# A hybrid attention/Fourier/Hyena layer: the Hyena filter constants loaded after the second modulation block, their products and sums one block later

## The chip, the cores and the metric

The kernel runs on one core of a Trainium2 chip. The metric is the device time of one execution in microseconds (us), the median of several runs. The engines of the core work side by side: TensorE (PE in the profile, its weight loads PEld), VectorE (DVE), ScalarE (ACT), GpSimd (POOL) and SyncE (SP), whose queue issues nearly all the loads here.

## The reference, cut to what matters

One layer for 128 context tokens and 256 latent tokens, width 2048, all in float32:

```python
ada = silu(cvec) @ w_ada + b_ada                 # 2048 x 6144: shift, scale, gate
h   = rmsnorm(x, norm_g) * (1 + scale) + shift
proj = h @ w_in                                  # attention, Fourier, Hyena inputs, gates
# Hyena branch: its long filters do not depend on x
f = sin(f_freq * (z @ f_w1 + f_b1)); f = sin(f_freq * (f @ f_w2 + f_b2))
f = (f @ f_w3) * exp(-t * deltas)                # f_w3: 64 x 2048; the decay window
f = f / (sum_t |f| + eps)                        # one sum for context, one for latents
kf = rfft(two-sided filter)                      # as products with DFT matrices here
y = x + gate * (merge(att, fourier, hyena(kf)) @ w_out)
```

## The kernel before

The products with the large weights are made in three passes of split float32 parts: each weight tile `w` (256 rows x 512 columns, 512 KB) is cast to `wh` on ACT (line 533) and its remainder `wl` taken on DVE (line 535); then `h_hi*wh`, `h_lo*wh` and `h_hi*wl` are summed. One such tile against all 384 tokens is a pair of row blocks, 24 matmuls of 384 columns for the Hyena columns.

The modulation (`ada`) is made in five blocks of its 2 x 2048 shift and scale columns (`ADA`, line 106): blocks 0 and 1 of 256 columns, blocks 2 to 4 of 512. Each block reads its part of `w_ada` (8 tiles of 512 KB in two DMAs each for blocks 0 and 1, 16 tiles of 512 KB for the others) through four buffers, two tiles to a step of matmuls (called an ada step below). Behind the last step a chain makes that block's `h`: a copy of the row (line 461), transposes on PE (464), bias and gain (474, 476), then per row block and token group one DVE instruction (485), one on ACT for `h_hi` (486) and one on DVE for `h_lo` (488). The end of a block is the event `h0` ... `h4`.

The first large products, of the Hyena columns (`hc_part`), go by `GROUPS` (line 108): group 0 needs only `h0` (four weight tiles), group 1 only `h1` (four), group 2 `h2` (eight), and so on; the partial sums of group 0 are copied out by ACT (line 695), those of the later groups added by DVE (line 697). Then come the Fourier columns (`u`), their gate (`gateB`), and the attention columns.

The filters (`filters`, line 599) are a flow of their own: two small sine layers, then the last layer's 12 products (line 626: two matmuls of 512 columns each, and a multiply by the decay window `win` on DVE, line 627), which need `f_w3` (`fw3`, two loads of 512 KB) cast and split in `split_w3` (lines 608, 609) and `win` (768 KB); the sums of absolute values (638), their reciprocals (640, 642), a spread of the row over all partitions (two matmuls for each of four rows, line 647, "spread rows" below) and a multiply (649); then six DFT steps with the split matrices `fwd_hi`, `fwd_lo` from the first 256 KB of `blob`. The Hyena convolution waits for `hc`, `filters` and `ada`; the attention columns wait for its first half (`conv0`).

All these flows are woven by a planner (`Weave`, lines 131 to 191) while the program is written: each step has an assumed cost on PE, a due time and events that it waits for; ready steps are taken by priority (ada 0, filters 2, Hyena 3, `main` 9). The order so found is the order of PE and of SP's queue; ACT and DVE are ordered by the scheduler of the framework after `h0`. An order once written is kept: an engine that waits for one instruction holds up all behind it.

Of the kernel before, what the change touches and what calls it, by code (L numbers as in the profile page):

```python
# [48 lines left out]
LATENT, CONTEXT = 0, 1  # L49
# [144 lines left out]
def step(pe, lat=0.0, after=(), wait=0.0, pace=0, count=0, at=0.0):  # L194
    return dict(pe=pe, lat=lat, after=after, wait=wait, pace=pace, count=count, at=at)
# [4 lines left out]
MM2 = 0.44  # L200
# [7 lines left out]
def hybrid_block(ctx: ExitStack, tc: tile.TileContext, a: dict):  # L208
# [28 lines left out]
    def tmp(name, shape=None, dt=F32):  # L237
        return work.tile(shape or [P, 512], dt, tag="tmp", name=name, bufs=6)

    def acc():  # L240
        return ps_acc.tile([P, 512], F32, tag="acc", name="acc")

    def aux():
        return ps_aux.tile([P, 512], F32, tag="aux", name="aux")

    def mm(out, lhsT, rhs, start=True, stop=True):
        nc.tensor.matmul(out, lhsT, rhs, start=start, stop=stop)  # L247
# [24 lines left out]
    def filter_constants(*which):  # L272
        for n in which:
            W.load((1, 1, 1.5, 0.5)[n] * LOAD)
            if n < 2:
                nc.sync.dma_start(out=fw3[n], in_=a["f_w3"][:, 1024 * n:1024 * n + 1024])
            elif n == 2:
                nc.sync.dma_start(out=win, in_=a["win"])
            else:
                nc.sync.dma_start(out=blob[:, 0:N_FWD], in_=a["blob"][:, 0:N_FWD])  # L280
# [127 lines left out]
    def ada_load():  # L408
        b, kt = next(ada_order, (None, None))
        if b is None:  # L410
            return
        _, c0, wd, *_ = (b, *ADA[b])
        nk = 512 // wd
        if b == 0 and kt // nk >= N_ADA:
            w = s6([P, nk, 2, wd], F32, "w_ada")
        else:
            w = adap.tile([P, nk, 2, wd], F32, tag="ada", name="w_ada", bufs=N_ADA)
        rows = w_ada[P * kt:P * kt + P * nk, 0:2 * D].rearrange("(k p) (t c) -> p k t c", p=P, t=2)
        for k in range(nk):
            nc.sync.dma_start(out=w[:, k], in_=rows[:, k, :, c0:c0 + wd])  # L420
        ada_loads.append((w, W.load(LOAD)))
# [3 lines left out]
    def ada(b, c0, wd, pace, rate):  # L425

        nk, nh, hw = 512 // wd, wd // 256, wd // 2
        pa = None
        n = 1 if b == 0 else 2
        if b == 0:  # L430
            for i in range(KT // nk):
                if i == KT // nk - 1:
                    prefetch(1)
                ada_load()
            prefetch(2)
            filter_constants(0, 1)
        if b == 1:
            yield step(0.0, pace=0.4)
            for _ in range(N_ADA):
                ada_load()  # L440
        for i in range(0, KT // nk, n):
            if b == 0 and i == 6:
                W.signal("ada0")
            yield step(0.26 + 0.43 * n * (nk * wd / 512), at=ada_loads[n - 1][1], pace=pace + rate * nk * i)
            pa = pa or acc()
            ws = [ada_loads.pop(0)[0] for _ in range(n)]
            for k in range(n * nk):
                kt = nk * i + k
                for j in range(4):
                    mm(pa[32 * j:32 * j + 32, 0:hw], cond[:, kt, :],  # L450
                       ws[k // nk][:, k % nk, j // 2, hw * (j % 2):hw * (j % 2) + hw], kt == 0, kt == KT - 1)
            if b > 0:
                for _ in range(n):
                    ada_load()
        if b == 0:
            ahead.append(weights(w_in, 0, OFF_HC))
            next(ahead[0])
        yield step(nh * TR, lat=0.6, after=("x",), wait=1.0)
        with tc.high_priority():
            row = tmp("ada_row")  # L460
            nc.vector.tensor_copy(out=row[:, 0:hw], in_=pa[:, 0:hw])
            pt = aux()
            for i in range(nh):
                nc.tensor.transpose(out=pt[:, P * i:P * i + P], in_=row[:, P * i:P * i + P], identity=ident)
            v = pt[:, 0:hw].rearrange("p (h t r q) -> p t q r h", h=nh, t=2, r=2)
            k0 = c0 // P
            ksl = slice(k0, k0 + wd // P)

            def rh(x):
                return x.rearrange("p (r h) -> p r h", r=2)  # L470

            for m, t, bias in ((am, 1, bsc), (sm, 0, bsh)):
                for s in range(2):
                    nc.vector.tensor_tensor(out=rh(m[:, s, ksl]), in0=v[:, t, s], in1=rh(bias[:, ksl]), op=ALU.add)
            for s in range(2):
                nc.vector.tensor_tensor(out=am[:, s, ksl], in0=am[:, s, ksl], in1=ng[:, ksl], op=ALU.mult)
            g = k0 // 4
            if k0 % 4 == 0:
                hh[g] = s6([P, 4, TOK], F32R, f"h{g}_hi")
                hl[g] = s6([P, 4, TOK], F32R, f"h{g}_lo")  # L480
            parts = [(xT[g][:, kt % 4, sl], hh[g][:, kt % 4, sl], hl[g][:, kt % 4, sl], rstd_b[:, sl],
                      am[:, s, kt:kt + 1], sm[:, s, kt:kt + 1])
                     for kt in range(k0, k0 + wd // P) for s, sl in ((LATENT, LSL), (CONTEXT, CSL))]
            for x, hi, lo, r, scale, shift in parts:
                nc.vector.scalar_tensor_tensor(out=x, in0=x, scalar=scale, in1=r, op0=ALU.mult, op1=ALU.mult)  # L485
                nc.scalar.activation(hi, x, AF.Identity, bias=shift)
            for x, hi, lo, r, scale, shift in parts:
                nc.vector.scalar_tensor_tensor(out=lo, in0=x, scalar=shift, in1=hi.bitcast(F32), op0=ALU.add,  # L488
                                               op1=ALU.subtract)
        if b == 0:  # L490
            ahead[0] = [next(ahead[0])]
        W.signal(f"h{b}")
# [24 lines left out]
    def prefetch(n):  # L517

        while len(loaded) < min(n, len(order)):
            src, kp, c0 = order[len(loaded)]  # L520
            w = stage.tile([P, 2, 512], F32, tag="w", name="w", bufs=N_W)
            nc.sync.dma_start(out=w, in_=src[256 * kp:256 * kp + 256, c0:c0 + 512].rearrange("(k p) c -> p k c", p=P))
            loaded.append((w, W.load(LOAD)))
# [75 lines left out]
    def filters():  # L599
# [13 lines left out]
        mm(p2[:, 0:TOK], fw2, f1)  # L613
        f2 = yield from sin_layer(p2, P, 10, "f2")
        f2s = split(f2, tmp("f2h", None, F32R)[:, 0:TOK], tmp("f2l", None, F32R)[:, 0:TOK])
        yield step(0.0, pace=0.1)
        filter_constants(2, 3)
        fw3s = [split_w3(x) for x in fw3]
        hw = [s6([P, NT, HW], F32, f"hw{j}") for j in range(4)]
        for jj, t in ((0, 0), (0, 1), (0, 2), (2, 0), (2, 1), (2, 2)):  # L620
            for j in (jj, jj + 1):
                yield step(MM2, lat=0.3, after=("h0",), wait=7.0)
                ph = aux()
                ts_, cs_ = slice(P * t, P * t + P), slice(512 * (j % 2), 512 * (j % 2) + 512)
                for i, f in enumerate(f2s):
                    mm(ph, f[:, ts_], fw3s[j // 2][:, cs_], i == 0, i == 1)
                nc.vector.tensor_tensor(out=hw[j][:, t, :], in0=ph, in1=win[:, t, :], op=ALU.mult)
        split(blob[:, 0:N_FWD].rearrange("p (q c) -> p q c", q=4), fwd_hi, fwd_lo)
        for s, ts in ((CONTEXT, (0,)), (LATENT, (1, 2))):
            pz = aux()  # L630
            for t in ts:
                yield step(0.0, lat=1.0)
                ab = [tmp("habs") for _ in range(4)]
                for j in range(4):
                    nc.scalar.activation(ab[j], hw[j][:, t, :], AF.Abs)
                yield step(1.0, lat=2.2, after=("h1" if s == CONTEXT else "h2",))
                for j in range(4):
                    mm(pz[32 * j:32 * j + 32, :], ones, ab[j], t == ts[0], t == ts[-1])
            r = tmp("hrec")
            nc.vector.tensor_scalar(out=r, in0=pz, scalar1=EPS, scalar2=None, op0=ALU.add)  # L640
            for c in range(4):
                nc.vector.reciprocal(out=r[:, P * c:P * c + P], in_=r[:, P * c:P * c + P])
            rh, rl = split(r, tmp("rh", None, F32R), tmp("rl", None, F32R))
            for j in range(4):
                yield step(MM2, lat=7.5 if j == 0 else 0.5)
                pb = aux()
                bcast_row(pb, 32 * j, rh, rl)
                for t in ts:
                    nc.vector.tensor_tensor(out=hw[j][:, t, :], in0=hw[j][:, t, :], in1=pb, op=ALU.mult)  # L649
# [507 lines left out]
```

## Time and profile before

| | us |
|---|---|
| median of 3 runs | 1303.23 (1303.11 to 1303.71) |
| the profiled execution | 1304.65, of which the span from first to last instruction 1302.9 |
| PE busy / DVE / ACT / POOL | 1282.2 (98%) / 736.9 (57%) / 469.3 (36%) / 27.6 (2%) |
| mean granted clock of PE | 0.997 |
| chain that ended last, by engine | PE 95%, DMA 2%, DVE 1%, ACT 1% |

PE bounds the kernel: a microsecond is gained or lost only where PE waits, or where its clock is at the lower level. The busy share of PE counts a matmul from its start to its modelled end, so it hides short waits; the waits are read from the order of the instructions in time.

### The profile page before, as it was taken

How to read it: one execution, taken by the hardware profiler on the slowest of the kernel's cores; microseconds unless marked ns; L12 is line 12 of the kernel's file. 1: busy time of each engine (PE TensorE's matmuls, PEld its weight loads, DVE VectorE, ACT ScalarE, POOL GpSimd, SP SyncE). 2: the span in 40 equal slices, each digit the busy share in tenths (PEclk: the TensorE clock that was granted, in tenths of full speed). 3: DMA queues.
4: the chain of work that ended last, by engine and by line, in shares of the span. 5: the costliest groups of instructions: out<-in, count | busy, mean ns of one | idle time of the engine just before them, and what ended most of it. 6: DMA issues, size and time to landing. Idle time of an engine off the chain costs nothing.

```text
span 1302.9 us, 16835 instructions
## 1 busy us (share of the span) xinstructions
PE 1282.2 (98%) x6602; PEld 1073.9 (82%) x6602; DVE 736.9 (57%) x1164; ACT 469.3 (36%) x736; POOL 27.6 (2%) x66
## 2 busy tenths in 40 slices
PE   7989999999999999999999999999999999999998
PEld 5857889889788988889888888888888888888886
DVE  4767767674775245542453766566656653454443
ACT  5432445322324344533444233323333333242221
POOL 0000000000000000000000000000000000010000
PEclk9999999999999999999999999999999999999999
DMA  9897853433434455444553555555555554464542
GB/s 337 299 324 268 278 179 114 116 111 97 113 97 138 146 125 114 123 132 123 124 110 114 180 176 171 185 170 178 173 183 161 176 157 129 141 189 133 157 150 86
DMA packets 118864, 210.95 MB, mean 162 GB/s; under 512 B 16385, under 2 KB 24961, under 8 KB 118785
## 3 DMA queue, kind: packets, MB, share of 16 engines
q1 hardware_dynamic: 116192, 202.13, 51.8%
q0 software_dynamic: 2448, 7.61, 1.8%
q8 instruction: 52, 0.85, 0.3%
q14 instruction: 28, 0.22, 0.1%
q10 hardware_dynamic: 144, 0.14, 0.0%
HBM read 205.65 MB, written 4.19 MB: 161 GB/s over the span
## 4 chain that ended last, share of the span: by engine, by line
PE 95%; DMA 2%; DVE 1%; ACT 1%; SPq 0%; issue 0%
PE acc L247 87%; PE aux L247 6%; DMA w_ada<-in_w_ada 2%; PE aux L846 0%; PE aux L1073 0%; PE aux L927 0%; SPq L365 0%; DVE hc L697 0%; DVE wl L535 0%; DVE h_lo L488 0%; PE aux L726 0%; ACT wh L533 0%; DVE xT L485 0%; SPq L420 0%; DVE hw L649 0%
## 5 line engine op out<-in xcount | busy, mean ns | idle before, releaser
L533 ACT CAST wh<-w 128x1024 fp32r<-128x1024 f32 x272 | 286.5, 1053 | 699.3 <-PE acc L247 634.7
L535 DVE TENSOR_TENSOR wl<-w,wh 128x1024 fp32r<-128x1024 f32 x272 | 332.3, 1223 | 364.1 <-PE acc L247 266.4
L247 PE MATMUL acc<-wh,h_hi 128*128 128x512 f32 x912 | 362.4, 397 | 0.6 <-ACT gateA L806 0.6
L247 PE MATMUL acc<-wh,h_lo 128*128 128x512 f32 x912 | 355.9, 390 | 0.0
L247 PE MATMUL acc<-wl,h_hi 128*128 128x512 f32 x912 | 240.0, 395 | 0.0
L247 PEld LDWEIGHTS acc<-wh,h_hi 128*128 128x128 f32 x912 | 171.3, 188 | 37.4 <-issue 1.4
L247 PEld LDWEIGHTS acc<-wh,h_lo 128*128 128x128 f32 x912 | 171.3, 188 | 35.7 <-issue 1.4
L247 PEld LDWEIGHTS acc<-wl,h_hi 128*128 128x128 f32 x912 | 168.6, 188 | 35.2 <-issue 1.9
L247 PE MATMUL acc<-h_lo,wh 128*128 128x384 f32 x448 | 151.3, 338 | 3.6 <-DVE h_lo L488 3.6
L247 PE MATMUL acc<-h_hi,wh 128*128 128x384 f32 x448 | 152.6, 341 | 0.1
L1008 DVE SCALAR_TENSOR_TENSOR gate_part<-w_gate,cond,gate_part 128x512 f32<-128x512 f32 x120 | 84.7, 749 | 27.2 <-DMA w_gate<-in_w_ada 27.2
L247 PE MATMUL acc<-h_hi,wl 128*128 128x384 f32 x448 | 91.9, 339 | 0.0
L247 PEld LDWEIGHTS acc<-h_hi,wh 128*128 128x128 f32 x448 | 84.5, 189 | 7.3 <-issue 5.5
L247 PEld LDWEIGHTS acc<-h_lo,wh 128*128 128x128 f32 x448 | 84.6, 189 | 5.6 <-DVE h_lo L488 4.7
L247 PEld LDWEIGHTS acc<-h_hi,wl 128*128 128x128 f32 x448 | 78.3, 188 | 5.9 <-issue 3.6
L247 PE MATMUL acc<-wh,m_hi 128*128 128x512 f32 x192 | 75.0, 390 | 0.0
L247 PE MATMUL acc<-wh,m_lo 128*128 128x512 f32 x192 | 74.7, 389 | 0.0
L247 PE MATMUL acc<-wl,m_hi 128*128 128x512 f32 x192 | 49.6, 390 | 0.0
L247 PEld LDWEIGHTS acc<-wh,m_lo 128*128 128x128 f32 x192 | 36.1, 188 | 7.4
L247 PEld LDWEIGHTS acc<-wh,m_hi 128*128 128x128 f32 x192 | 36.0, 188 | 7.4
L247 PEld LDWEIGHTS acc<-wl,m_hi 128*128 128x128 f32 x192 | 36.0, 188 | 7.4
L697 DVE TENSOR_TENSOR hc<-acc,hc 128x384 f32<-128x384 f32 x64 | 31.5, 550 | 16.8 <-PE acc L247 16.7
(253 smaller groups left out, 1197.7 us busy)
## 6 DMA issues: line engine op xcount, KB each, us to landing
w<-in_w_in SPq DMA_DIRECT2D x208, 512.0 KB, 3.8
w_ada<-in_w_ada SPq DMA_DIRECT2D x48, 512.0 KB, 5.7
w<-in_w_br SPq DMA_DIRECT2D x32, 512.0 KB, 4.1
w_gate<-in_w_ada SPq DMA_DIRECT2D x64, 256.0 KB, 4.2
w<-in_w_out SPq DMA_DIRECT2D x32, 512.0 KB, 3.9
w_ada<-in_w_ada SPq DMA_DIRECT2D x32, 256.0 KB, 7.0
x<-in_x_sample SPq DMA_DIRECT2D x4, 512.0 KB, 8.8
bm<-in_rpb SPq DMA_DIRECT2D x32, 64.0 KB, 7.4
```

Source lines behind the costliest of these rows:

```text
L247: nc.tensor.matmul(out, lhsT, rhs, start=start, stop=stop)
L533: nc.scalar.copy(out=wh, in_=w)
L535: nc.vector.tensor_tensor(out=wl, in0=w, in1=wh.bitcast(F32), op=ALU.subtract)
L697: nc.vector.tensor_tensor(out=hc[i][:, j, :], in0=ps, in1=hc[i][:, j, :], op=ALU.add)
L1008: nc.vector.scalar_tensor_tensor(out=part[s], in0=w, scalar=cond[:, kt, s:s + 1], in1=before, op0=ALU.mult, op1=ALU.add)
```

## The change

The loads of `fw3` are taken out of block 0 of the modulation, and all four constant loads (`fw3` twice, `win`, `blob`; 2 MB) are issued by the filters' flow 0.5 planned us after `h1`. The 12 products wait for `h1` plus 17 planned us where they waited for `h0` plus 7. The context's sums wait for `h2` (before `h1`), the latents' for `h3` (before `h2`). The diff in full:

```diff
@@ -433,7 +433,6 @@
                     prefetch(1)
                 ada_load()
             prefetch(2)
-            filter_constants(0, 1)
         if b == 1:
             yield step(0.0, pace=0.4)
             for _ in range(N_ADA):
@@ -613,13 +612,13 @@
         mm(p2[:, 0:TOK], fw2, f1)
         f2 = yield from sin_layer(p2, P, 10, "f2")
         f2s = split(f2, tmp("f2h", None, F32R)[:, 0:TOK], tmp("f2l", None, F32R)[:, 0:TOK])
-        yield step(0.0, pace=0.1)
-        filter_constants(2, 3)
+        yield step(0.0, after=("h1",), wait=0.5)
+        filter_constants(0, 1, 2, 3)
         fw3s = [split_w3(x) for x in fw3]
         hw = [s6([P, NT, HW], F32, f"hw{j}") for j in range(4)]
         for jj, t in ((0, 0), (0, 1), (0, 2), (2, 0), (2, 1), (2, 2)):
             for j in (jj, jj + 1):
-                yield step(MM2, lat=0.3, after=("h0",), wait=7.0)
+                yield step(MM2, lat=0.3, after=("h1",), wait=17.0)
                 ph = aux()
                 ts_, cs_ = slice(P * t, P * t + P), slice(512 * (j % 2), 512 * (j % 2) + 512)
                 for i, f in enumerate(f2s):
@@ -633,7 +632,7 @@
                 ab = [tmp("habs") for _ in range(4)]
                 for j in range(4):
                     nc.scalar.activation(ab[j], hw[j][:, t, :], AF.Abs)
-                yield step(1.0, lat=2.2, after=("h1" if s == CONTEXT else "h2",))
+                yield step(1.0, lat=2.2, after=("h2" if s == CONTEXT else "h3",))
                 for j in range(4):
                     mm(pz[32 * j:32 * j + 32, :], ones, ab[j], t == ts[0], t == ts[-1])
             r = tmp("hrec")
```

## Rows read from the trace of the kernel before

**Rows 1.** Stretches: us; busy us (instructions) of PE, PEld, DVE, ACT, POOL; clock; DMA share; GB/s.
```profile
95.00:100.00 5.00, 2.52 (x7) 1.96 (x7) 4.41 (x11) 0.80 (x2) 0.00 (x0) 0.65 0.95 259
100.00:105.00 5.00, 5.00 (x33) 2.48 (x33) 1.26 (x2) 0.00 (x0) 0.00 (x0) 0.67 0.83 292
```

**Rows 2.** PE in time, around h2: start, us, line, operation [idle before, releaser].
```profile
87.61 1.29 PE L247 MATMUL acc<-w_ada,cond 128*32 128x256 f32 x16
...
89.95 1.07 PE L247 MATMUL aux<-habs,ones 128*32 128x512 f32 x8
...
97.48 0.69 PE L247 MATMUL acc<-h_lo,wh 128*128 128x384 f32 x1 [3.25 <-DVE h_lo L488]
```

**Rows 3.** DVE in time, around h2.
```profile
88.97 0.42 DVE L461 COPY ada_row<-acc 128x256 f32<-128x256 f32 x1 [1.32 <-PE acc L247]
...
93.03 1.95 DVE L697 TENSOR_TENSOR hc<-acc,hc 128x384 f32<-128x384 f32 x4 [0.43 <-PE acc L247]
94.90 1.22 DVE L535 TENSOR_TENSOR wl<-w,wh 128x1024 fp32r<-128x1024 f32 x1
...
96.69 2.72 DVE L488 SCALAR_TENSOR_TENSOR h_lo<-xT,sm,h_hi 128x256 fp32r<-128x256 f32 x8
```

**Rows 4.** PE in time, around h1.
```profile
57.35 0.43 PE L247 MATMUL acc<-w_ada,cond 128*32 128x128 f32 x8 [0.32 <-DMA w_ada<-in_w_ada]
...
58.52 0.27 PE L464 MATMUL aux<-first,ada_row 128*128 128x128 f32 x1
...
60.58 1.66 PE L247 MATMUL acc<-h_hi,wl 128*128 128x384 f32 x8
```

**Rows 5.** PE in time, the context's spread rows.
```profile
68.73 0.50 PE L247 MATMUL aux<-rh,ident_r 128*128 128x512 f32 x1 [1.11 <-ACT rh L308]
69.46 0.50 PE L247 MATMUL aux<-rl,ident_r 128*128 128x512 f32 x1 [0.23 <-DVE rl L309]
```

**Rows 6.** SP's queue in time: the filter loads and block 1's first loads.
```profile
22.72 0.94 SPq L276 DMA_DIRECT2D fw<-in_f_w  x2
...
27.67 9.49 SPq L420 DMA_DIRECT2D w_ada<-in_w_ada  x8
```

**Rows 7.** Stretches: the hole in the loads.
```profile
41.00:46.00 5.00, 5.00 (x52) 4.17 (x51) 4.55 (x7) 2.87 (x6) 0.00 (x0) 1.00 0.39 123
```

**Rows 8.** PE in time, around h0 (matmuls on `first` alone are fillers).
```profile
27.35 0.72 PE L247 MATMUL acc<-w_ada,cond 128*32 128x128 f32 x16
...
30.79 0.44 PE L247 MATMUL acc<-h_hi,wh 128*128 128x384 f32 x1
31.54 0.44 PE L247 MATMUL acc<-h_lo,wh 128*128 128x384 f32 x1 [0.31 <-DVE h_lo L488]
```

**Rows 9.** PE in time, one filter product between two pairs of group 0's matmuls.
```profile
42.14 0.39 PE L247 MATMUL aux<-fw3hl,f2h 128*128 128x512 f32 x1
...
42.60 0.51 PE L247 MATMUL acc<-h_hi,wl 128*128 128x384 f32 x2
```

**Rows 10.** The instructions on tile hw: duration ns min/median/max, first and last start.
```profile
L627 DVE TENSOR_TENSOR hw<-aux,win x12: 684/692/693, 38.6 to 51.2; 128x512 f32<-128x512 f32 x12
```

**Rows 11.** DVE in time, the latents' reciprocals.
```profile
103.71 0.69 DVE L640 TENSOR_SCALAR hrec<-aux 128x512 f32<-128x512 f32 x1 [4.30 <-PE aux L247]
...
109.63 0.69 DVE L309 TENSOR_TENSOR rl<-hrec,rh 128x512 fp32r<-128x512 f32 x1 [0.69 <-ACT rh L308]
```

**Rows 12.** The instructions on tiles hc and specC, as rows 10.
```profile
L697 DVE TENSOR_TENSOR hc<-acc,hc x64: 547/548/558, 66.6 to 235.0; 128x384 f32<-128x384 f32 x64
...
L683 ACT COPY specC<-aux x2: 570/571/572, 160.0 to 200.2; 1x512 f32<-1x512 f32 x2
```

**Rows 13.** PE in time, the transposes of block 3.
```profile
138.56 0.38 PE L464 MATMUL aux<-first,ada_row 128*128 128x128 f32 x2
```

**Rows 14.** The chain that ended last: start, us, what (the end of `conv0`).
```profile
302.46 1.34 PE aux L247 x12
303.79 7.98 PE acc L247 x46
```

## The prediction

> **What bounds the kernel now.** I read first the page's busy shares and the chain that ended last: PE carries the end nearly everywhere, so only PE's waits and its clock count. Then I read PE's busy time and clock by stretches and the instructions in time where PE is not full. The reader should see that past 32 us PE loses time in few places, and that nearly all the large ones lie before 105 us, where the change works. They are: at the last ada step of block 1 PE waits 0.3 us for `w_ada` [rows 4]; at the context's spread rows 1.1 + 0.2 us for the reciprocals [rows 5]; at `h2` 3.25 us for `h_lo` [rows 2]. [...] Together 0.3 + 1.3 + 3.25 + 2.9 = 7.8 us. That is all that the change can win there.
>
> The `h2` wait has a cause worth seeing. The chain from the row copy (88.97) to the first `h_lo` that PE needs (97.48) is 8.5 us long because DVE, in its written order, first waits for and adds group 1's last sums (0.43 + 1.95) and makes a `wl` (1.22) [rows 3]. Without them it is 8.5 - 3.6 = 4.9 us.
>
> **What the change does, part by part.**
>
> *Loads.* 2 MB leave SP's queue ahead of block 1 (the fw loads stand at 22.7, block 1's at 27.7) [rows 6] and stand behind block 2's first four tiles. Of their own they cost PE nothing: the queue has a hole of about 3 us here, a DMA share of 0.39 over five us [rows 7], because block 1's next loads wait for PE to free buffers. Block 1 is ready sooner, and its DMA wait (0.3 us) goes. The same bytes still stand ahead of block 2's last tile, so `h2` gains little from the loads. They can't delay the products, which are due 17 planned us after `h1`; behind SP's four issues only block 2's and the weights' loads queue, and those have four tiles ahead.
>
> *Products.* 12 at 42.60 - 42.14 = 0.46 us [rows 9] are 5.5 us of PE work that leave the stretch from `h0` to `h1` and enter that from `h1` to `h2`. PE's sum is the same; only the holes count.
>
> *The hole at `h1`.* Going through the planner's costs by hand, block 1's last ada step now comes after all of group 0 (before, group 0's last `wl` products stood behind it and, with the context's sums and an ada step, covered the chain: group 0 ends at 60.58 + 1.66 = 62.2, with no idle time noted on the way from 57.8 [rows 4]). Nothing ready is left: group 1 needs `h1`, the products are not due, block 2's first step stands behind group 1's first matmuls. The chain's length is read at `h0`, where fillers cover it: from the end of the ada step (27.35 + 0.72) to the first matmul that needs `h_lo` (31.54) is 3.5 us [rows 8]. Less the transposes (0.27) and one early matmul, about 3.0 us of new idle. From below, 1.5 if the scheduler and a late load let group 0's matmuls fall behind; from above 4.5, the way from that ada step's end to group 1 before (57.78 to 62.24) [rows 4]. I take 3.0, from the nearest row, an equal chain.
>
> *From `h1` to `h2`.* Group 1, eight ada steps, and now the products. DVE has to multiply each product by the window (12 x 0.69 = 8.3 us) [rows 10] where in group 0 it had little else; in group 1 it also adds the sums (0.55 each, four to a weight tile) [rows 12] and makes `wl` (1.22) [rows 3]. By their due times the products run beside two weight tiles: 8.3 + 8 x 0.55 + 2 x 1.22 = 15.1 us of DVE, against 2 x 24 x 0.173 (7.98 us for 46 matmuls) [rows 14] + 5.5 = 13.8 us of PE, or 15.1 with one ada step of 1.3 [rows 2] among them. DVE falls behind by 1.3 us or not at all, and PE waits where its auxiliary PSUM buffers run out. Bounds 0 and 2.5 (two such overhangs); I take 0.6, the middle of the first two.
>
> *The hole at `h2`.* By the plan all of group 1 and all products are done before block 2's last two ada steps, so DVE's chain is free of the two foreign pieces: 4.9 us (above), of which PE fills 0.4 with transposes [rows 13], 1.1 with the context's sums and 1.3 with block 3's first step [rows 2]. 2.1 us of idle in place of 3.25. Bounds: 1 (more cover left) and 5 (the foreign pieces again).
>
> *Sums.* The context's spread rows move behind `h2`. Their chain on DVE starts only after the longer `h2` chain. From the first reciprocal instruction to `rl` it takes 109.63 + 0.69 - 103.71 = 6.6 us [rows 11]; it can begin when the last `h_lo` is done, 2.0 us after PE restarts (six of eight instructions in 2.72) [rows 3]; PE reaches the spread rows 6.5 us after its restart (line 645 has them 7.5 planned us behind the sums, which end 1.0 after `h2`, and group 2 starts 2.0 after it). So PE waits about 2 + 6.6 - 6.5 = 2.1 for `rl`, and a little more for what DVE interleaves: I take 2.6 (bounds 0.5 and 4), where it was 1.3 at `h1` [rows 5]. The latents' spread rows behind `h3` meet a full group 2 and the same chain as before: nothing either way, up to 1.
>
> *Clock.* A hole of 3.25 us brought 6.8 us of half speed [rows 1, 2]; a wait of 1.3 us [rows 5] brought none, as the page's mean clock of 0.997 has room for little beside that spell. The new holes of 3.0, 2.1 and 2.6 lie between. I take one spell, 2.9 us (bounds none, and two: 5.8).
>
> [...]
>
> **The sum.** New: 3.0 + 0.6 + 2.1 + 2.6 + 2.9 = 11.2; gone: 7.8; so 3.4 us longer. On the profiled execution's 1304.65 that gives 1308.0; this one lies 1.4 over the median, so for the median 1303.2 + 3.4 = 1306.6.
>
> **The rivals.**
>
> *No spell of low clock.* The same holes, all too short or too broken. For it: only one of two waits in the trace was followed by a spell. Against: three holes, not one. 11.2 - 2.9 - 7.8 = 0.5 us longer: 1303.7.
>
> *Faster: the products cover `h2` and the holes shrink.* If group 1's last matmuls or some products slip behind block 2's last ada step, they stand beside the chain, as group 1's did before, while DVE's foreign pieces are gone; `h1` comes with some of group 0 left, and the spread rows wait no more than before. 1.5 + 0 + 1.5 + 1.3 = 4.3 and no spell, against 7.8: 3.5 us less, 1299.7. It decides from the point where block 1's last tile lands before group 0's last weight tile is done in PE's order, so that about 1.5 us of work is behind it. For it: block 1's loads start some 5 us sooner [rows 6]. Against: the order is fixed by planned times, not by when loads land.
>
> *Two spells, or the filters come too late.* The latents' sums move from 89.95 to about 138.6 [rows 2, 13], 49 us, less some 9 of stall and half speed that lay in the chain before; filters that were done at 200 would be done at about 240, against the last sums of `hc` at 235.0 [rows 12]. The Hyena branch then starts some 5 us late. Its first half has 8.0 us of `main`'s work left behind it [rows 14], after which PE would have nothing but the attention columns, and they wait for `conv0`. So 5 us are hidden; past 8 each further us is lost on PE. With 3 lost there, or with a second spell: 1306.6 + 2.9 = 1309.5.
>
> *A queue held by a late filter load.* The casts of `fw3` (lines 608, 609) stand in ACT's and DVE's order; if they stand ahead of group 1's sums while `fw3` is still in flight, everything behind waits. Up to 2 us, inside the range above.
>
> **How the numbers follow.** One spell, 1306.6: 0.40. No spell, 1303.7: 0.28. Faster, 1299.7: 0.17. Two spells or late filters, 1309.5: 0.15. A measurement of this kernel can tell about 0.2%, 2.6 us, from no change. Each case has an error of some 2 us: of the first, six tenths lie over 1305.8; of the second, eight tenths lie within; of the third, seven tenths lie under 1300.6. Faster 0.12 + 0.03 = 0.15; slower 0.24 + 0.03 + 0.15 = 0.42; within 0.43. The range takes in most of the third and the fourth: 1299.6 to 1310.4. The likeliest case's own range is 1304.6 to 1308.6.
>
> **What would show it.** PE's order should have all of group 0 ahead of block 1's last ada step, and then a wait of about 3 us for `h_hi` and `h_lo`, near 54 to 57 us, where before it was full. Group 1 should begin about 5 us sooner than at 62.2. The last ada step of block 2 should stay near 88 to 91, with DVE's chain behind it near 5 us and no `hc` or `wl` inside it; the spread rows should wait 2 to 3 us near 103. From 250 us on every instruction of `main` should be later by one and the same amount. It is wrong if the `h1` hole is under 1.5 us, if the granted clock stays at 1.00 up to 110 us, if DVE holds PE for more than 2.5 us among the products, or if PE waits between 300 and 320.

## The result, and the profile after

| | before | changed |
|---|---|---|
| median, us | 1303.47 (1303.11 to 1304.45) | 1311.27 (1310.13 to 1311.54) |
| ratio | | 1.0053, 95% interval 1.0042 to 1.0065 |
| profiled execution, and its span | 1304.65, 1302.9 | 1311.54, 1309.8 |
| PE busy | 1282.2 | 1284.2 |

The change costs 0.5%, 6.9 us by the ratio (the two medians differ by 7.8): slower, as forecast, but about twice the 3.4 us of the sum. That is the upper end of the range: 1.0053 times the 1303.2 of the forecast is 1310.1, against 1310.4, and the median itself lies 0.9 past it. Matmul by matmul, the large products of the two profiles stand 6.9 us apart from the last sums of `hc` (near 240 us) to the end; beyond 200 us PE's two longest waits are the same in both (0.7 for `pT`, 0.6 for `gateA`), none between 300 and 320. So all of it was lost ahead of the Fourier columns, and the reading goes by the places of the forecast.

PE around `h1` in the changed kernel (start, us, line, operation, idle before and its releaser); it answers to [rows 4]:

```profile
52.96 1.08 PE L247 MATMUL acc<-w_ada,cond 128*32 128x128 f32 x32
54.60 0.33 PE L463 MATMUL aux<-first,ada_row 128*128 128x128 f32 x1 [0.57 <-DVE ada_row L460]
56.81 0.44 PE L247 MATMUL acc<-h_hi,wh 128*128 128x384 f32 x1 [1.88 <-ACT h_hi L485]
57.56 0.45 PE L247 MATMUL acc<-h_lo,wh 128*128 128x384 f32 x1 [0.31 <-DVE h_lo L487]
```

0.57 + 1.88 + 0.31 = 2.8 us of idle, where group 0's last products had stood beside the chain. The line numbers of the changed kernel are lower by one here.

PE around `h2` and at the context's spread rows; it answers to [rows 2] and [rows 5]:

```profile
89.10 1.07 PE L247 MATMUL acc<-w_ada,cond 128*32 128x256 f32 x16
91.77 0.64 PE L247 MATMUL acc<-w_ada,cond 128*32 128x256 f32 x8 [1.60 <-DMA w_ada<-in_w_ada]
93.08 0.64 PE L247 MATMUL acc<-w_ada,cond 128*32 128x256 f32 x8 [0.67 <-DMA w_ada<-in_w_ada]
94.27 0.44 PE L463 MATMUL aux<-first,ada_row 128*128 128x128 f32 x2 [0.55 <-DVE ada_row L460]
...
96.92 0.64 PE L247 MATMUL acc<-w_ada,cond 128*32 128x256 f32 x8 [0.66 <-DMA w_ada<-in_w_ada]
...
98.65 0.44 PE L247 MATMUL acc<-h_lo,wh 128*128 128x384 f32 x1 [0.72 <-DVE h_lo L487]
...
107.93 0.50 PE L247 MATMUL aux<-rl,ident_r 128*128 128x512 f32 x1 [1.04 <-DVE rl L309]
```

DVE in the same stretch:

```profile
93.78 0.43 DVE L460 COPY ada_row<-acc 128x256 f32<-128x256 f32 x1 [1.90 <-PE acc L247]
...
100.49 0.69 DVE L639 TENSOR_SCALAR hrec<-aux 128x512 f32<-128x512 f32 x1
...
107.19 0.68 DVE L309 TENSOR_TENSOR rl<-hrec,rh 128x512 fp32r<-128x512 f32 x1
```

The chain behind `h2` is short (from the row copy, 93.78, to the first `h_lo` on PE 4.9 us, against 8.5) and PE's idle pieces in it are 0.55 + 0.66 + 0.72 = 1.9 us. But ahead of it block 2's last step now waits 1.60 + 0.67 = 2.3 us for its two tiles.

Stretches (us; busy us and instructions of PE, PEld, DVE, ACT, POOL; clock; DMA share; GB/s); they answer to [rows 1]:

```profile
55.00:60.00 5.00, 2.84 (x17) 1.26 (x20) 3.16 (x14) 1.50 (x4) 0.00 (x0) 0.84 0.91 314
60.00:65.00 5.00, 5.00 (x39) 3.60 (x32) 1.22 (x1) 2.35 (x3) 0.00 (x0) 0.82 1.03 411
...
95.00:100.00 5.00, 3.57 (x29) 1.49 (x22) 5.00 (x19) 2.88 (x8) 0.00 (x0) 0.93 0.94 295
100.00:105.00 5.00, 5.00 (x32) 3.90 (x32) 4.56 (x7) 0.36 (x1) 0.00 (x0) 0.72 0.78 243
```

Two spells at the lower level, 0.50 (so in each microsecond from 59 to 61 and from 100 to 102 us, and 1.00 again from 62 and from 103), in place of one: (0.16 + 0.18) x 5 x 2 = 3.4 us behind `h1`, (0.07 + 0.28) x 5 x 2 = 3.5 us behind `h2`, with PE at work throughout, so some 1.7 us lost by each.

The latents' spread rows, where the forecast had put "nothing either way, up to 1". PE:

```profile
143.10 1.04 PE L247 MATMUL aux<-habs,ones 128*32 128x512 f32 x8
...
152.19 0.34 PE L247 MATMUL acc<-h_lo,wh 128*128 128x384 f32 x1
154.77 0.50 PE L247 MATMUL aux<-rh,ident_r 128*128 128x512 f32 x1 [2.25 <-ACT rh L308]
155.50 0.50 PE L247 MATMUL aux<-rl,ident_r 128*128 128x512 f32 x1 [0.22 <-DVE rl L309]
```

And DVE in the same stretch; it answers to [rows 11]:

```profile
142.56 2.72 DVE L487 SCALAR_TENSOR_TENSOR h_lo<-xT,sm,h_hi 128x256 fp32r<-128x256 f32 x8
145.19 0.69 DVE L639 TENSOR_SCALAR hrec<-aux 128x512 f32<-128x512 f32 x1
145.79 1.22 DVE L534 TENSOR_TENSOR wl<-w,wh 128x1024 fp32r<-128x1024 f32 x1
146.94 2.57 DVE L641 RECIPROCAL hrec<-hrec 128x128 f32<-128x128 f32 x3
150.12 1.95 DVE L696 TENSOR_TENSOR hc<-acc,hc 128x384 f32<-128x384 f32 x4 [0.62 <-PE acc L247]
151.99 1.22 DVE L534 TENSOR_TENSOR wl<-w,wh 128x1024 fp32r<-128x1024 f32 x1
153.12 0.95 DVE L641 RECIPROCAL hrec<-hrec 128x128 f32<-128x128 f32 x1
154.75 0.69 DVE L309 TENSOR_TENSOR rl<-hrec,rh 128x512 fp32r<-128x512 f32 x1 [0.69 <-ACT rh L308]
```

PE is done with the sums at 144.1 and at the rows at 152.5, 8.4 us later. DVE begins only when `h3`'s last `h_lo` is done (145.2), and from there to the end of `rl` (155.4) it needs 10.2 us, because two `wl`, and group 2's sums with a wait for them, stand between the reciprocals. In the kernel before the last of the same sums ends at 103.6 (101.75 + 1.83, below) and the rows begin 8.3 us later, but the chain started at 103.71 and took 6.6 us [rows 11]: 1.5 us to spare. Only the last of the four rows waited there, 0.53 us for a multiply by DVE.

```profile
101.75 1.83 PE L247 MATMUL aux<-habs,ones 128*32 128x512 f32 x8
...
111.84 0.50 PE L247 MATMUL aux<-rh,ident_r 128*128 128x512 f32 x1
...
116.48 0.50 PE L247 MATMUL aux<-rh,ident_r 128*128 128x512 f32 x1 [0.53 <-DVE hw L649]
```

The sum as the two profiles have it. New: `h1` 2.8, block 2's tiles 2.3, `h2` 1.9, the context's rows 1.0, the latents' rows 2.5, clock 3.4: 13.9. Gone: the 7.8 of the forecast, 0.5 that the latents' rows waited before, and two short waits for `w_ada` that the forecast left out, 0.19 us at 56.6 and 0.36 at 91.8. That makes 5.0 us; another 0.3 is a later first product (31.12 against 30.79), and 1.6 of the 6.9 is not assigned.

Two theories fit so far. Theory A: each hole in PE's order has a price of its own, and the prices add; the largest new ones are 2.8, 2.5 and 2.3. Theory B: the loads set the pace. Block 2's last tile lands at 93.03 where it landed at 88.22, the DMA share is 0.78 to 1.05 in all stretches from 55 to 110 us, and what PE idles elsewhere only takes up that lateness.

### The profile page after: what moved, and what is told of

Its sections match the earlier page's. It is cut to its first block, busy times and chain, and to the rows that moved or that the text cites. A ratio compares the mean times of both kernels' runs of the same rounds, so it can differ in the third digit from the quotient of the medians.

```text
span 1309.8 us, 16828 instructions
## 1 busy us (share of the span) xinstructions
PE 1284.2 (98%) x6602; PEld 1075.1 (82%) x6602; DVE 736.9 (56%) x1164; ACT 469.7 (36%) x736; POOL 27.6 (2%) x66
## 4 chain that ended last, share of the span: by engine, by line
PE 94%; DMA 2%; DVE 2%; ACT 1%; issue 1%; SPq 0%; DVEq 0%
PE acc L247 86%; PE aux L247 6%; DMA w_ada<-in_w_ada 2%; DMA x<-in_x_prompt 1%; DVE wl L534 0%; PE aux L845 0%; PE aux L1072 0%; DVE xT L484 0%; PE aux L926 0%; ACT wh L532 0%; DVE h_lo L487 0%; PE aux L725 0%; DVE hc L696 0%; PE aux L463 0%; DVE rl L309 0%
## 5 line engine op out<-in xcount | busy, mean ns | idle before, releaser
L247 PE MATMUL acc<-w_ada,cond 128*32 128x256 f32 (+1 forms) x640 | 37.5, 350 | 4.5 <-DMA w_ada<-in_w_ada 4.5
```

## The experiments

All ratios are to the kernel before, timed beside them. (The kernel before in these comparisons: 1304.2 to 1304.4 us.)

**One part at a time, and two mends.**

The sums alone:

```diff
-                yield step(1.0, lat=2.2, after=("h1" if s == CONTEXT else "h2",))
+                yield step(1.0, lat=2.2, after=("h2" if s == CONTEXT else "h3",))
```

> The kernel before with the sums alone moved (context behind h2, latents behind h3); loads and products stay. Theory A (each hole in PE's order has its own price and the prices add): the latents' rows wait 2.5 us behind h3 in place of 0.5, the context's about 1.0 in place of 1.3, and h1 loses 1.1 us of cover: 2 to 3.5 us over the kernel before, 1305.5 to 1307. Theory B (the loss is the late delivery of block 2's last tile, and the rest takes up the same time): nothing of the delivery changes here, so at most 2 us, all of it behind h3, and block 2's last tile still lands near 88.2 us.

Measured: 1312.27, ratio 1.0055 (1.0043 to 1.0067). Both theories missed: the sums alone, with loads and products where they were, cost as much as the whole change. The latents' rows wait 2.23 + 0.22 us again, and here a spell of half clock follows them:

```profile
150.00:155.00 5.00, 2.77 (x16) 2.32 (x14) 4.27 (x7) 0.62 (x1) 0.00 (x0) 1.00 0.91 299
155.00:160.00 5.00, 4.78 (x26) 2.66 (x26) 1.79 (x4) 0.00 (x0) 0.00 (x0) 0.66 0.24 64
```

In all this profile has 13.7 us at the lower level from 55 to 115 and from 140 to 160 us, where the kernel before has 6.8, and its waits from 50 to 200 us add up to 10.0 us in place of 6.7.

The changed kernel with its loads put back (the first line in block 0 of the modulation); products and sums late:

```diff
+            filter_constants(0, 1)
...
-        yield step(0.0, after=("h1",), wait=0.5)
-        filter_constants(0, 1, 2, 3)
+        yield step(0.0, pace=0.1)
+        filter_constants(2, 3)
```

> The changed kernel with its loads put back (fw3 ahead of block 1, window and matrices ahead of its first tiles); products and sums stay late. Theory A with the prediction's step that the loads cost PE nothing of their own: the time stays within 2.5 us of the changed kernel's 1311.3 (only the 2.3 us wait ahead of block 2's last step can go), and a wait of about 3 us for h_hi stays at h1. Theory B (late delivery): block 2's last tile lands near 88 us in place of 93.0, and the time falls by 4 us or more, to 1307 or less. Third: without products to do, PE runs out of work before block 1's tiles are there, waits for w_ada there for 4 us or more, and the time rises over 1312.

Measured: 1310.48, ratio 1.0049 (1.0037 to 1.0061). Theory B falls: the waits for `w_ada` up to `h2` are 3.1 us in sum where they were 2.9, only at other places (the longest, 2.0, at block 1's last steps at 53.9), `h2` has 2.9 us for `h_lo` again, and the time is the changed kernel's within what can be told, some 2 us. PE starved at block 1 as the third expectation said, but for 2.9 us and not 4, and not to over 1312. The changed kernel's own trace agrees: block 2's last tile takes no longer from its issue to its landing (86.17 to 93.03, 6.9 us) than before (81.48 to 88.22, 6.7); it is issued later, behind the ada step at 85.00 (before: 80.31), and behind the ada step at 89.10 PE has nothing else left to do.

The changed kernel with the latents' sums back behind `h2`:

```diff
-                yield step(1.0, lat=2.2, after=("h2" if s == CONTEXT else "h3",))
+                yield step(1.0, lat=2.2, after=("h2",))
```

> The changed kernel with the latents' sums back behind h2 (the context's stay behind h2 too). If the 2.5 us wait for the latents' rows behind h3 is a price of its own: 2.0 us less than the changed kernel (a wait of 0.5 stays, as in the kernel before), 1309.3. If it only takes up time that another wait would take, or if eight sums in a row at h2 make a new one: no gain, 1311 or more, with a wait for rh or rl of over 2 us somewhere else.

Measured: 1313.50, ratio 1.0062 (1.0048 to 1.0075), no gain. The rows' wait at 155 us is gone, and PE waits 3.07 us for the row copy of `h3` instead (it is busy in 1.93 of the 5 us from 140): DVE has the latents' work in front of it there, in the order that is shown below for the run with the context's sums alone.

The changed kernel with fillers in the idle pieces (`keep_warm(n)` makes n matmuls of the identity with 128 columns; first ahead of block 2's last step, then behind the transposes):

```diff
+            if b == 2 and i == KT // nk - n:
+                keep_warm(12)
...
+            if b in (1, 2):
+                keep_warm({1: 13, 2: 8}[b])
```

> The changed kernel with 13 small matmuls without use behind h1's transposes, 12 ahead of block 2's last step and 8 behind h2's transposes, in PE's order where it waits now. If the two spells of half clock come from those idle pieces: the granted clock stays at 1.00 from 55 to 110 us, 3.4 us less, 1307.9. If the fillers push the work behind them back by as much, or if the clock falls all the same: 1311 or more.

Measured: 1311.24, ratio 1.0054 (1.0042 to 1.0066). The clock half of it came as expected: 1.00 in all stretches from 55 to 110 us. The time did not fall. The fillers were too many: each takes some 0.23 us (13 in 3.07 us behind `h1`'s transposes), so 33 are 7.6 us where 2.2 + 2.3 + 1.4 = 5.9 us had been idle, and at the latents' rows the same wait (2.23 us) was followed by a spell (155 to 160 us: 0.66). The granted clock is 0.998 or 0.999 in all five executions, where it is 0.996 or 0.997 in the four of the changed kernel, so what the clock gave was taken up again, by the fillers or by waits that moved; on the price of a spell this run is inconclusive.

**The two halves of the sums' move, and the place of the rows.**

The kernel before with the context's sums alone late:

```diff
-                yield step(1.0, lat=2.2, after=("h1" if s == CONTEXT else "h2",))
+                yield step(1.0, lat=2.2, after=("h2",))
```

> The kernel before with the context's sums alone moved behind h2 (the latents' stay behind h2, loads and products stay). If the two halves of the sums' move add up: h1 loses the cover of 1.1 us and gets a wait of 1.5 us with a spell of half clock of 3.4 us (1.7 lost), the rows' waits hardly change: 3 us over the kernel before. If instead the context's chain on DVE pushes the latents' and h3's chain back, as in the changed kernel with the latents' sums put back: a wait of 3 us for the row copy at h3, and 6 us or more over the kernel before.

Measured: 1311.64, ratio 1.0055 (1.0042 to 1.0068). The second expectation holds. DVE in its order, and PE's step that waits:

```profile
136.95 3.07 DVE L649 TENSOR_TENSOR hw<-hw,aux 128x512 f32<-128x512 f32 x5
139.94 0.68 DVE L661 TENSOR_TENSOR ev<-hw,hw 128x512 f32<-128x512 f32 x1
141.08 1.02 DVE L697 TENSOR_TENSOR hc<-acc,hc 128x384 f32<-128x384 f32 x2 [0.45 <-PE acc L247]
142.02 0.68 DVE L662 TENSOR_TENSOR hw<-hw,hw 128x512 f32<-128x512 f32 x1
142.62 0.69 DVE L309 TENSOR_TENSOR evod<-ev,evod 128x512 fp32r<-128x512 f32 x1
143.38 0.69 DVE L309 TENSOR_TENSOR ol<-hw,evod 128x512 fp32r<-128x512 f32 x1
143.99 0.42 DVE L461 COPY ada_row<-acc 128x256 f32<-128x256 f32 x1
```

```profile
139.42 1.07 PE L247 MATMUL acc<-w_ada,cond 128*32 128x256 f32 x16
144.46 0.44 PE L464 MATMUL aux<-first,ada_row 128*128 128x128 f32 x2 [3.07 <-DVE ada_row L461]
```

The latents' multiplies and the first pieces for the DFT stand ahead of `h3`'s row copy.

The kernel before with the latents' sums alone late:

```diff
-                yield step(1.0, lat=2.2, after=("h1" if s == CONTEXT else "h2",))
+                yield step(1.0, lat=2.2, after=("h1" if s == CONTEXT else "h3",))
```

> The kernel before with the latents' sums alone moved behind h3 (the context's stay behind h1, loads and products stay). If the halves add up: h1 is as in the kernel before, the latents' rows wait 2.4 us behind h3 (0.5 before), and a spell of half clock of 3.4 us follows: 2 us over the kernel before without that spell, 3.7 with it. Rival: the rows wait only because the context's chain was late as well; then within 0.7 us of the kernel before.

Measured: 1309.21, ratio 1.0037 (1.0024 to 1.0050), 4.8 us. The wait for the rows is there without the context's move, so the rival falls; it is followed by more half clock than expected:

```profile
151.08 0.79 PE L247 MATMUL aux<-rh,ident_r 128*128 128x512 f32 x1 [2.24 <-ACT rh L308]
```

```profile
150.00:155.00 5.00, 3.92 (x18) 2.35 (x22) 2.36 (x4) 0.62 (x1) 0.00 (x0) 0.58 0.32 119
155.00:160.00 5.00, 5.00 (x26) 3.97 (x19) 2.82 (x5) 1.05 (x1) 0.52 (x1) 0.74 0.73 233
```

(0.42 + 0.26) x 10 = 6.8 us of it, which begin 4.2 us ahead of 155, at 150.8; PE idles up to 151.08, so 6.5 are at work and 3.3 lost. With 2.24 - 0.53 = 1.7 for the wait that is 5.0, against 4.8 measured. And the halves do not add: 4.8 and 7.2, together 7.2 in the first run.

The changed kernel with the latents' rows later:

```diff
-                yield step(MM2, lat=7.5 if j == 0 else 0.5)
+                yield step(MM2, lat=(7.5 if s == CONTEXT else 11) if j == 0 else 0.5)
```

> The changed kernel with the latents' first spread row 11 planned us behind the sums in place of 7.5, so that PE has some 3 us more of the Hyena columns ahead of it. If the 2.5 us wait is DVE's chain alone, it goes and no spell follows: 2.5 to 4 us less than the changed kernel, 1307 to 1309. If DVE only has other work put in front (it is nearly full there) or the later filters cost the same at the Hyena branch: within 1 us of 1311.

Measured: 1305.60, ratio 1.0009 (1.0000 to 1.0019). This one number takes back 5.7 us (0.44%) of the 6.9, more than expected. DVE's chain is as long as it was; PE only comes to it later and waits for nothing:

```profile
143.60 0.69 DVE L639 TENSOR_SCALAR hrec<-aux 128x512 f32<-128x512 f32 x1
...
153.16 0.69 DVE L309 TENSOR_TENSOR rl<-hrec,rh 128x512 fp32r<-128x512 f32 x1 [0.69 <-ACT rh L308]
```

```profile
154.06 0.40 PE L247 MATMUL aux<-rh,ident_r 128*128 128x512 f32 x1
154.29 0.40 PE L247 MATMUL aux<-rl,ident_r 128*128 128x512 f32 x1
```

```profile
95.00:100.00 5.00, 3.45 (x31) 1.68 (x24) 5.00 (x18) 2.87 (x8) 0.00 (x0) 1.00 1.02 383
100.00:105.00 5.00, 5.00 (x39) 3.89 (x37) 4.96 (x8) 1.52 (x2) 0.00 (x0) 1.00 0.64 213
...
155.00:160.00 5.00, 5.00 (x38) 3.91 (x37) 5.00 (x8) 0.00 (x0) 0.52 (x1) 1.00 0.74 270
```

The wait of PE's first DFT step for `evod` (0.7 us, near 197 us) is gone as well. 2.5 + 0.7 = 3.2 us are waits. The rest is open. A spell of half clock behind the rows is part of it in other runs: of the five executions profiled with this wait (the changed kernel and four of the runs above), four show one, of 3.4 us or more (1.7 to 3.3 us lost); of the four with later rows none does. But the changed kernel's own profile is the one of the five without, and its granted clock is 0.996 or 0.997 in all four executions, no lower than the 0.997 that the eleven with later rows have in the mean (0.994 to 0.998). So the clock does not explain the rest here. Some 2.5 us are not assigned; the difference of the two ratios itself is known to about 2 us. Ahead of 105 us these two kernels are the same, and yet the first of block 2's last two tiles is waited for 1.60 us in the one profile and 0.49 in the other, and the spell behind `h2` is in the one and not in the other: the two profiles differ by more than the edit.

One control is missing: the kernel before with its latents' rows at 11. It waits 0.5 us at those rows and 0.7 for `evod`, so up to 1.2 us of the 5.7 might be had there too, without the change.

**The kernel before, mended.**

The fillers stand once, ahead of group 2's first matmul with `h_lo`:

```diff
-                yield step(MM2, lat=7.5 if j == 0 else 0.5)
+                yield step(MM2, lat=10 if j == 0 else 0.5)
...
         def product(ps, j, kt, px, w, start, stop):
+            if (c0, kps, kt, j, px) == (OFF_HC, GROUPS[2][1], 2 * kps[0], 0, 1) and stop is False and not warmed:
+                warmed.append(keep_warm(12))
```

> The kernel before with the spread rows 10 planned us behind the sums in place of 7.5, and 12 small matmuls without use (0.23 us each, 2.7 us in all) between group 2's first h_hi and its first h_lo, in the 3.3 us in which PE waits at h2. If idle time brings the spell of half clock and the rows' wait is a matter of their place: the clock stays at 1.00 up to 110 us and the rows wait for nothing: 1.3 + 2.9 = 4 us less than the kernel before, ratio 0.997. If the later rows push something else back, or the clock falls all the same: within 1.5 us of the kernel before.

Measured: 1301.66, ratio 0.9979 (0.9971 to 0.9988), 2.7 us less. The clock is 1.00 in all stretches from 55 to 165 us. A wait of 0.99 us for `rl` is left at the context's rows, so most of the gain is the spell's: 2.9 us in the forecast. The granted clock agrees: 0.9993 in the mean of its eleven executions, 0.9976 in the 21 of the kernel before beside them; 0.0017 of 1304 us is 2.2 us, as an estimate. The rows did not wait for nothing, as the first expectation had it, so its 4 us did not come.

**With the rows out of the way.** Three more with `lat` 11 for the latents' rows. First the changed kernel with fillers at the same places as above, but fewer:

```diff
+                keep_warm(6)
...
+                keep_warm({1: 8, 2: 5}[b])
```

> The changed kernel with the latents' rows 11 planned us behind their sums, and fillers (0.23 us each) that fit the idle pieces: 8 behind h1's transposes, 6 ahead of block 2's last step, 5 behind h2's transposes. If the spells of half clock behind h1 and h2 come from these idle pieces and cost what half the time in them is: the clock stays at 1.00 from 55 to 110 us, and the time is 1.7 to 3.4 us less than with the rows alone (ratio 1.0009): ratio 0.9983 to 0.9996. If the clock spells cost nothing on the path, or the fillers take as much: ratio 1.0005 to 1.0015.

Measured: 1305.03, ratio 1.0004 (0.9996 to 1.0013). Clock 1.00 throughout from 55 to 110 us; 0.6 us less than without fillers, which can't be told from none. It lies between the two expectations. Here 19 x 0.23 = 4.4 us of fillers take the place of idle pieces of about the same sum. The granted clock is 0.999 or 1.000 in all eleven executions, against 0.994 to 0.998 without fillers, so the clock was won, and most of what it gave was taken up again, by the fillers or by waits that moved; which of them, this run does not show.

Then the changed kernel with its loads put back, and the rows later:

> Products and sums late as in the changed kernel, the latents' rows 11 planned us behind their sums, but the loads where the kernel before has them. It differs from the changed kernel with later rows by the loads alone. If moving the loads costs nothing of its own (the prediction): within 1 us of it, ratio near 1.001. If late loads hold up block 2's last tile: 1.5 to 2.3 us less, ratio 0.9993. If early loads with late products starve PE at block 1's last steps (5 us of idle there by the plan): ratio 1.002 to 1.004.

Measured: 1306.23, ratio 1.0015 (1.0005 to 1.0025). The first expectation holds: the loads cost nothing that can be told. PE waits for block 1's last tiles, but 1.9 us in all and not 5.

And the kernel before with the sums alone late, and the rows later:

> The kernel before with the sums alone moved, and the latents' rows 11 planned us behind theirs. If the rows' wait with the spell behind it and the wait for evod were the greater part of the 7.2 us that the sums alone cost: 4.5 to 5.5 us less than those, ratio 1.0015 to 1.002. If they were not: ratio 1.004 or more.

Measured: 1305.43, ratio 1.0006 (0.9998 to 1.0015), 6.4 us less than with the rows at 7.5, somewhat more than expected.

The three steps of the change, with the rows where they were and later:

| | latents' rows at 7.5 | at 11 |
|---|---|---|
| sums late | 1.0055 | 1.0006 |
| sums and products late | 1.0049 | 1.0015 |
| sums, products and loads late (the change) | 1.0053 | 1.0009 |

Down a column nothing moves by more than the intervals (each entry +-0.0010 to 0.0012). Across, each row loses 0.34 to 0.49%, 4.4 to 6.4 us. So the place of the latents' rows against DVE's chain behind `h3` is the greater part of the loss, with its waits and, where a spell follows, that; moving products and loads costs nothing that can be told, within about 2 us. That their new holes are paid for by the ones that go is how the sums above read it; no run takes them apart.

Last, the mended kernel before with the context's rows later still:

```diff
-                yield step(MM2, lat=10 if j == 0 else 0.5)
+                yield step(MM2, lat=(13 if s == CONTEXT else 10) if j == 0 else 0.5)
```

> The mended kernel before (12 fillers at h2), with the context's spread rows 13 planned us behind their sums in place of 10; the latents' stay at 10. A wait of 1.0 us for rl was left at the context's rows with 10: if it goes, 1 us less, ratio 0.997. If DVE puts other work in front again: ratio 0.998 as with 10.

Measured: 1300.01, ratio 0.9971 (0.9961 to 0.9980): 3.8 us less than the kernel before, and better than the changed one by 0.8%. The wait at the context's rows is gone. PE at `h2`, the fillers in the hole, and the stretches of [rows 1]:

```profile
92.93 0.34 PE L247 MATMUL acc<-h_hi,wh 128*128 128x384 f32 x1
93.11 2.84 PE L247 MATMUL aux<-first 128*128 128x128 f32 x24
96.54 0.44 PE L247 MATMUL acc<-h_lo,wh 128*128 128x384 f32 x1 [0.60 <-DVE h_lo L492]
```

```profile
95.00:100.00 5.00, 4.36 (x40) 2.57 (x38) 3.46 (x11) 0.80 (x2) 0.00 (x0) 1.00 0.78 277
100.00:105.00 5.00, 5.00 (x41) 4.02 (x38) 4.63 (x6) 1.05 (x1) 0.00 (x0) 1.00 0.83 290
```

The hole at `h2` is as long as it was (2.84 us of fillers and 0.60 of idle, where 3.25 us had been idle); only its aftermath at half clock is gone (1.00 in both stretches, where it was 0.65 and 0.67). Against the mend with 10 this is 1.0 us less, as expected, but the two intervals overlap.

## Why the prediction was right or wrong

**The step that failed** is the one sentence on the latents: "The latents' spread rows behind `h3` meet a full group 2 and the same chain as before: nothing either way, up to 1." A full group 2 was the trouble, not the cover. At `h2` PE itself waits for the chain of `h2`, so that DVE is free when the sums come (it idles 4.3 us ahead of 103.71) and the chain has 1.5 us to spare in PE's 8.3. At `h3` PE has group 2 and does not wait; it reaches the rows in the same 8.4 us while DVE still makes `h3` and serves group 2 (10.2 us, and 1.1 later). I had taken 6.6 us from [rows 11] without asking what filled DVE around it, though it was the question that I had asked of the same chain at `h2`. With the rows out of the way the change costs 1.2 us (0 to 2.5), under the forecast's 3.4; with them 6.9. So the way was forecast right, but in good part by luck: the terms of the sum, 11.2, came to 9.1, and what made the change clearly slower are two terms that the sum did not have, 2.5 at the latents' rows and 2.3 for block 2's tiles.

**The hole at `h1`:** 2.8 where 3.0 was forecast, by an equal chain read at `h0`. All of group 0 stands ahead of block 1's last step, and group 1 begins 5.4 us sooner than 62.2, all as written.

**From `h1` to `h2`:** 0.6 was taken for DVE behind on the products. PE waited for it nowhere among them: 0. But the sum missed that block 2's last tiles would be late: 2.3 us for DMA. "`h2` gains little from the loads" and "Of their own they cost PE nothing" hold in the time, within some 2 us (the second and third line of the table), not in the place: with early loads the waits for `w_ada` are as long in sum (3.1 us against 2.9), and the longest (2.0) lies at block 1.

**The hole at `h2`:** 1.9 where 2.1 was forecast; the chain on DVE without foreign pieces 4.9 us, as forecast.

**The context's rows:** 1.0 where 2.6 was forecast (1.3 before). The chain on DVE was longer than the 6.6 us taken, 7.4 (from 100.49 to the end of `rl`, 107.87), and began 1.8 us behind PE's restart at 98.65; but PE, slowed by the half clock (3.5 us of it), came to the second matmul of the rows 8.2 us after its restart and not 6.5: 1.8 + 7.4 - 8.2 = 1.0. In the profile of the changed kernel with later rows, which has no spell here (1.00 in both stretches from 95 to 105 us), the rows wait 0.8.

**Clock:** one spell, 2.9 us lost, was taken; it was two of 3.4 us, 3.4 lost. The 2.9 is an estimate from [rows 1], which no run times by itself: clocks of 0.65 and 0.67 over five microseconds each are (0.35 + 0.33) x 5 x 2 = 6.8 us at half clock, of which PE idles about 1 and works 5.8, losing 5.8 / 2 = 2.9; the trace of the kernel before has 0.50 in each microsecond from 97 to 103 us. The three shorter holes did not prevent half clock: 6.9 us of half clock in sum in the profile of the changed kernel, against the 6.8 of the one long hole. With fillers in the idle pieces the clock is at 1.00: in all stretches from 55 to 110 us of the changed kernel with 33 and with 19 of them, from 55 to 165 us of the kernel before with 12.

**The rivals.** "No spell" and "faster" did not come. Of "two spells, or the filters come too late" the second spell came, as part of a different sum; the filters were done at 240 us, as that rival had it, and still PE waited for nothing between 300 and 320, nor did the later rows cost anything there. No wait for a late filter load is in the trace either: all four had landed by 65.8 us.

## What to carry to other kernels

A step that is moved from one event to another meets the work that the engines have there. For each chain that another engine waits for, read both ends at the new place: when the making engine becomes free and what its order puts between the chain's links, and how soon the waiting engine comes by; where the waiting engine used to be held up too, the chain had a cover that does not move along. Before a change is judged, try its due times: here one of them (7.5 to 11) was worth 5.7 us, where the change with it set so costs 1.2.

## What the runs showed of the hardware

The same idle was not always followed by half clock. The wait at the latents' rows, 2.23 to 2.25 us, was followed by none in one execution (the changed kernel's: 1.00 in all stretches from 145 to 165 us), by 3.4 us in three and by 6.8 in one more; up to 105 us the changed kernel and the one with later rows run the same program, with idle pieces of 1.60, 0.67, 0.55, 0.66, 0.72 and of 0.49, 0.66, 0.55, 0.81, 0.70 us around `h2`, the first with a spell behind them (0.93 and 0.72 in the two stretches from 95 to 105 us) and the second with none (1.00 in both). What decides between the two is not shown. And dummy matmuls were worth their place in a hole that they did not shorten: 12 of 0.23 us in the hole at `h2`, with the spread rows at 10, brought 2.7 us (1.6 to 3.8), most of it by the clock (2.2 us, the estimate above). In the changed kernel 33 and 19 of them kept the clock up as well (1.00 from 55 to 110 us) and brought nothing that can be told.
